# Attention scores from three products of 64 rows a head, two heads side by side on TensorE's row halves

## The chip, the cores and the metric

The kernel runs on one core of one Trainium2 chip. A core has a matrix engine (TensorE, "PE" in the profile), a vector engine (VectorE, "DVE"), an activation engine (ScalarE, "ACT"), a general engine (GpSimd, "POOL"), a queue engine that mostly issues DMAs (SyncE, "SP"), an on-chip memory of 128 partitions (SBUF) and eight accumulator banks (PSUM) into which TensorE writes. The metric is the device time of one execution in microseconds; smaller is better. Shown times are medians of several runs.

A product on TensorE loads a stationary operand (up to 128 rows of contraction by 128 columns) and streams a moving operand (the same rows by up to 512 columns) through it. "64 rows" below means that the contraction runs over 64 partitions only, so the product uses half of the array's rows; the other half can hold the stationary operand of another product. "Column halves" are the same thing for an output of 64 partitions.

## What is computed

Two layers of a transformer over 512 latent tokens and 256 context tokens, D = 1024. Layer 0 has 8 neighbourhood-attention heads (called NA) and 8 latent-attention heads (MLA) side by side, layer 1 has 16 sliding-window heads (SWA) that share 2 key/value heads. Cut to the attention scores:

```python
# NA (layer 0), head dim 64: near keys with a bias, and all context keys, in one softmax
s_lat = einsum('bnqhd,bknmhd->bhnqkm', qr, k_blk) * scale + bias;  s_ctx = einsum('bnqhd,bchd->bhnqc', qr, kc) * scale
# MLA (layer 0): 64 features of the head's own and 32 rotary ones, whose keys all heads share
sc = einsum('bqhc,bkc->bhqk', q_lat, c_kv) + einsum('bqhr,bkr->bhqk', q_rope, k_rope)
# SWA (layer 1): query head h uses key/value head h // 8; a sink logit per head joins the softmax
s_ctx = einsum('bqkgd,bckd->bkgqc', qg, kc) * scale;  s_lat = einsum('bqkgd,bmkd->bkgqm', qg, kb) * scale
```

Everything is float32. The kernel splits an operand x into a high part h (x rounded to TensorE's float32r type) and a low part l = x - h, and takes a product as h·h + l·h + h·l.

## The kernel before

**Stages.** Modulation vectors, the first input projections, then NA (about 197 to 275 us of the span), MLA (275 to 404 us), output projection and feed-forward of layer 0, then projections and SWA of layer 1 (about 1026 to 1178 us), output projection and feed-forward of layer 1. Inside a program stage the order on each engine comes from a scheduler that simulates the program and sorts by priority; a few stretches are ordered by hand, but not the attention.

**Attention jobs.** A job takes two lanes (for NA and SWA the two heads of a pair; for MLA two query groups of one head) through: scores into a PSUM bank of tag `s` (there are three), `take` (VectorE adds the bias, negates, copies to SBUF and keeps the minimum), `exps` (ScalarE), `turned` (transposes of 128x128 blocks by TensorE, copied back by VectorE and ScalarE), and `weighted`, the products with the values (L532 before, L531 after), where the lanes sit on the two column halves. Jobs overlap by one (`attend`), and side work (projections, finishing of pairs) is stepped between them. A query tile is 128 tokens, numbers 0 to 3 latent, 4 and 5 context.

**Scores of NA and SWA before** (`stacked_scores`, L745 and L746). A head's stationary operand is 128 rows: its 64 high rows and its 64 low rows, stacked. The moving operand is twice the head's keys: high over high, and low over low. So two products of 128 rows give all four terms. To make these, `put_q` writes high and low on different partition halves for each head, and `put_k` writes each key part twice, either by computing it again or by four DMAs a pair (`copies`).

**Scores of MLA before** (`latent_operands`, L1065 to L1067). A head's high tile holds its 64 own rows and 32 rotary rows, its low tile likewise; three products of 96 rows (head 0 of a pair) or 128 rows (head 1, with 32 rows of zeros). ScalarE and GpSimd build these tiles a head at a time (L1055, L1056), the rotary rows come by DMA on SP's queue.

**Queues.** All weight and bias loads and the on-chip copies named above are issued by `dma` (L134) on SP's queue, in the order that the scheduler gave. NA's bias tiles (`nb`) have two buffers, so a bias is loaded when the one before it has been read.

Of the kernel before, what the change touches and what calls it, by code (L numbers as in the profile page):

```python
# [10 lines left out]
F32R = mybir.dt.float32r  # L11
AF = mybir.ActivationFunctionType
ALU = mybir.AluOpType
# [42 lines left out]
ORDER = ("2", "n3", "m", "")  # L56
AFTER = "012k5678"
DBG = 0.43
KC = (0, 1, 0)
# [3 lines left out]
RK, RQ, RL, SQ = (2, 0), (0, 0), (0, 0), 1  # L63
# [37 lines left out]
def hybrid_kernel(ctx: ExitStack, tc, I, out):  # L101
# [443 lines left out]
    class Head:  # L545


        def __init__(self, side, scores, v, reach, bias, start, sums, mins):
            self.side, self.scores, self.v, self.reach, self.bias, self.start = side, scores, v, reach, bias, start
            self.dn = lambda q: sums[:, q, side : side + 1]  # L550
            self.mx = lambda q: mins[:, q, side : side + 1]
# [3 lines left out]
    def latent_lane(h, qs, blocks):  # L555

        sc = PS("s")
        for i, n in enumerate(qs):
            h.scores(sc[:, i * NX : (i + 1) * NX], n, CTXS)
        for i, n in enumerate(qs):  # L560
            a, z = h.reach(n)
            w = (z - a) * P
            s = PS("s")[:, :w]
            h.scores(s, n, slice(a * P, z * P))
            pt[0] += 1
            p = B(tag=PT[phase[0]][pt[0] % len(PT[phase[0]])])
            take(p, slice(w, w + NX), sc[:, i * NX : (i + 1) * NX], zeros.to_broadcast([P, NX]), h.start, h.mx(n))
            take(p, slice(0, w), s, h.bias(n), h.mx(n), h.mx(n))
            exps(p, slice(0, w + NX), h.mx(n), h.dn(n))
            for j, kt in enumerate([*range(a, z), 4, 5]):  # L570
                blocks[n, kt] = p[:, j * P : (j + 1) * P]
            yield True

    def near_lane(h, qs, blocks):

        for n in qs:
            s = PS("s")
            for at, key, w in NEAR[n]:
                h.scores(s[:, at : at + w], n, slice(key, key + w))
            pt[0] += 1  # L580
            p = B(tag=PT[phase[0]][pt[0] % len(PT[phase[0]])])
            take(p, slice(0, 512), s, h.bias(n), h.start, h.mx(n))
            exps(p, slice(0, 512), h.mx(n), h.dn(n))
            for j, kt in enumerate(NEAR_TILES[n]):
                blocks[n, kt] = p[:, j * P : (j + 1) * P]
            yield True

    def context_lane(h, qs, blocks):

        sc, p = PS("s"), B(tag="p")  # L590
        for i, n in enumerate(qs):
            c = slice(i * NX, (i + 1) * NX)
            h.scores(sc[:, c], n, CTXS)
            take(p, c, sc[:, c], zeros.to_broadcast([P, NX]), -LOWEST, h.mx(n))
            exps(p, c, h.mx(n), h.dn(n))
            for j in range(2):
                blocks[n, 4 + j] = p[:, i * NX + j * P : i * NX + (j + 1) * P]
        yield True

    def job(lanes, use, then=None):  # L600

        all_blocks = [{} for _ in lanes]
        for (h, qs), blocks in zip(lanes, all_blocks):
            yield from (context_lane if qs[0] > 3 else latent_lane if h.reach else near_lane)(h, qs, blocks)
        yield False
        o = PO()
        yield from weighted(o, [(h.v, blocks, qs) for (h, qs), blocks in zip(lanes, all_blocks)])
# [4 lines left out]
    def pair_jobs(hs, po, ctx_q, then):  # L612

        for qs in (((4, 5),) if ctx_q else ()) + ((0, 1), (2, 3)):
            c = slice(qs[0] * P, qs[0] * P + NX)
            yield job([(h, qs) for h in hs], lambda o, c=c: S.copy(po[:, c], o), then if qs[0] == 2 else None)

    def head_jobs(h, po, then):

        r = slice(64 * h.side, 64 * h.side + 64)  # L620
# [1284 lines left out]
```

## Time and profile before

| what | value |
|---|---|
| median of 3 runs | 1587.41 us (1586.18 to 1589.96) |
| the profiled execution: time, span | 1591.88 us, 1589.8 us |
| PE busy | 1536.5 us, 97% of the span |
| DVE, ACT, POOL busy | 1182.3, 806.8, 225.8 us |
| granted PE clock, mean | 0.992 |
| score products NA and SWA (L745, L746) | 216 and 216 |
| score products MLA (L1065, L1066, L1067) | 80 each |

The span is the time from the first to the last instruction that the profiler recorded; the execution's own time is 2.1 us longer. "Busy" counts a matmul until its modelled end, so neighbouring matmuls overlap and 97% does not mean that the array streams 97% of the time; start-to-start distances say how long a product holds the array.

### The profile page before, as it was taken

To read this page: it belongs to the slowest core of one execution; us is meant where nothing else is said; L and a number is where in the kernel's file an instruction comes from. 1 tells how busy PE (TensorE), PEld (TensorE's weight loads), DVE (VectorE), ACT (ScalarE), POOL (GpSimd) and SP (SyncE) were. 2 spreads that over 40 slices of the span, in tenths; PEclk is the share of its full clock that TensorE was granted. 3 is DMA by queue.
4 is the path that set the end of the run, shared out by engine and by line. 5 is a ranking of instruction groups with operands and counts; after the bars stand their busy time and mean duration, and the time that the engine had idled before them with its cause. 6 is when DMAs were issued, how large, how long until landed. Compare 5 with 4: busy or idle time off the path is not lost.

```text
span 1589.8 us, 26694 instructions
## 1 busy us (share of the span) xinstructions
PE 1536.5 (97%) x10034; PEld 1373.0 (86%) x10034; DVE 1182.3 (74%) x2365; ACT 806.8 (51%) x1643; POOL 225.8 (14%) x218
## 2 busy tenths in 40 slices
PE   6998989999999999999999999999999999999998
PEld 4686877787898989899999999878889998898997
DVE  4495968668589778785877776868877778687686
ACT  4364487677366324242333345557756545354463
POOL 0151724230010000000001010393002000000000
PEclk9999999999999999999999999999999999999999
DMA  9445343101562564746556555131006133233232
GB/s 342 148 162 192 102 125 101 36 11 64 180 208 86 163 233 154 240 144 214 199 191 243 194 208 207 41 104 43 2 14 198 40 108 128 87 100 114 90 103 87
DMA packets 80465, 214.93 MB, mean 135 GB/s; under 512 B 10192, under 2 KB 17872, under 8 KB 80336
## 3 DMA queue, kind: packets, MB, share of 16 engines
q1 hardware_dynamic: 73552, 188.05, 36.3%
q0 software_dynamic: 4480, 22.02, 3.6%
q10 hardware_dynamic: 2304, 3.15, 0.5%
q8 instruction: 79, 1.29, 0.3%
q14 instruction: 50, 0.41, 0.1%
HBM read 186.97 MB, written 23.07 MB: 132 GB/s over the span
## 4 chain that ended last, share of the span: by engine, by line
PE 76%; DVE 10%; DMA 7%; issue 3%; ACT 2%; POOL 2%; SPq 0%; DVEq 0%; ACTq 0%; POOLq 0%
PE pso L532 5%; PE pss L320 4%; PE pss L321 3%; PE pss L322 3%; PE pss L1343 3%; PE pss L1342 3%; PE pss L1341 3%; PE psd L320 3%; PE psd L321 3%; PE psd L322 3%; PE psd L1341 3%; PE psd L1343 3%; PE psd L1342 3%; PE pst L1343 3%; PE pst L1341 3%
## 5 line engine op out<-in xcount | busy, mean ns | idle before, releaser
L307 ACT CAST wh<-wr 128x512 fp32r<-128x512 f32 (+2 forms) x142 | 108.3, 777 | 196.3 <-DMA wr<-in_w_dn_dram 35.7
L308 DVE TENSOR_TENSOR wl<-wr,wh 128x1024 fp32r<-128x1024 f32 (+2 forms) x139 | 128.4, 931 | 75.4 <-ACT wh L307 74.8
L538 ACT ACTIVATE p<-p,sm 128x512 f32<-128x512 f32 (+3 forms) x144 | 105.1, 730 | 27.5 <-DVE sm L542 24.8
L215 DVE CUSTOM_DVE_ANT_0 p<-rope,cond 128x1024 bf16<-128x1024 f32 x64 | 77.5, 1222 | 29.8 <-DMA rope<-in_mod_w_dram 26.2
L321 PE MATMUL psd<-b,wh 128*128 128x256 f32 (+4 forms) x257 | 88.2, 343 | 0.0
L1343 PE MATMUL pss<-b,wl 128*128 128x256 f32 (+1 forms) x258 | 80.2, 311 | 4.2 <-DVE wl L1329 4.2
L1521 POOL DMA_DIRECT2D home<-p x40 | 21.6, 540 | 437.5 <-DVE p L1166 434.9
L1342 PE MATMUL pss<-b,wh 128*128 128x256 f32 (+1 forms) x258 | 80.0, 310 | 0.0
L320 PE MATMUL psd<-b,wh 128*128 128x512 f32 (+4 forms) x217 | 78.4, 361 | 1.4 <-ACT b L430 0.7
L1341 PE MATMUL pss<-b,wh 128*128 128x256 f32 (+1 forms) x258 | 79.6, 309 | 0.0
L320 PE MATMUL pss<-st,wh 128*128 128x256 f32 (+2 forms) x231 | 78.0, 338 | 0.4 <-ACT wh L307 0.4
L532 PE MATMUL pso<-ph,b 128*64 128x256 f32 (+1 forms) x384 | 78.1, 362 | 0.3 <-DVE ph L470 0.2
L532 PE MATMUL pso<-pl,b 128*64 128x256 f32 (+1 forms) x384 | 77.6, 362 | 0.7 <-DVE pl L470 0.7
L322 PE MATMUL pss<-st,wl 128*128 128x512 f32 (+2 forms) x231 | 77.8, 337 | 0.0
L322 PE MATMUL psd<-b,wl 128*128 128x512 f32 (+4 forms) x217 | 76.5, 353 | 0.0
L1343 PE MATMUL pst<-b,wl 128*128 128x384 f32 (+1 forms) x240 | 74.4, 311 | 0.3 <-DVE wl L1329 0.3
L1342 PE MATMUL pst<-b,wh 128*128 128x384 f32 (+1 forms) x240 | 74.4, 310 | 0.0
L1341 PE MATMUL pst<-b,wh 128*128 128x384 f32 (+1 forms) x240 | 74.4, 310 | 0.0
L321 PE MATMUL pss<-b,wh 128*128 128x256 f32 (+4 forms) x227 | 74.2, 328 | 0.1
L1342 PE MATMUL psd<-b,wh 128*128 128x384 f32 (+1 forms) x222 | 69.8, 314 | 0.0
L1341 PE MATMUL psd<-b,wh 128*128 128x384 f32 (+1 forms) x222 | 69.6, 314 | 0.0
L1343 PE MATMUL psd<-b,wl 128*128 128x384 f32 (+1 forms) x222 | 69.6, 314 | 0.0
(624 smaller groups left out, 5349.6 us busy)
## 6 DMA issues: line engine op xcount, KB each, us to landing
wr<-in_w_gu_dram SPq DMA_DIRECT2D x88, 512.0 KB, 4.2
rope<-in_mod_w_dram SPq DMA_DIRECT2D x48, 512.0 KB, 3.7
wr<-in_w_out_dram SPq DMA_DIRECT2D x32, 512.0 KB, 3.6
wr<-in_w_dn_dram SPq DMA_DIRECT2D x64, 256.0 KB, 2.8
p<-home SPq DMA_DIRECT2D x40, 384.0 KB, 3.9
home<-p POOLq DMA_DIRECT2D x40, 384.0 KB, 5.0
wr<-in_w_in_dram SPq DMA_DIRECT2D x21, 512.0 KB, 4.1
st<-in_mod_wp_dram SPq DMA_DIRECT2D x32, 256.0 KB, 4.7
```

The lines of the kernel that those rows point to most:

```text
L215: V.tensor_tensor_reduce(out=T("p", [P, D], mybir.dt.bfloat16), in0=w, in1=cond[:, v, :], op0=ALU.mult, op1=ALU.add, scale=1.0, scalar=0.0 ...
L307: S.copy(h, r)
L308: (G if eng else V).tensor_tensor(lo, r, f(h), op=ALU.subtract)
L320: PE.matmul(o, wh[:, k], mh[:, c], start=first and k == 0, stop=False)
L321: PE.matmul(o, wh[:, k], ml[:, c], start=False, stop=False)
L322: PE.matmul(o, wl[:, k], mh[:, c], start=False, stop=last and k == n - 1)
L532: ins = PE.matmul(o[64 * i : 64 * i + 64, c], v(kt), t, start=n == 0, stop=n == len(moving[i]) - 1)
L538: S.activation(p[:, c], p[:, c], AF.Exp, bias=nm, scale=-1.0, accum_out=dn)
L1341: PE.matmul(o, wh, xh, start=first and k == 0, stop=False, skip_group_check=not first)
L1342: PE.matmul(o, wh, xl, start=False, stop=False, skip_group_check=not first)
L1343: PE.matmul(o, wl, xh, start=False, stop=k == 3, skip_group_check=not first)
L1521: G.dma_start(home[m], t)
```

## The change

**NA and SWA.** Queries and keys of a pair of heads are kept as they come out of the projection: one tile with the high parts of both heads (head 0 in partitions 0 to 63, head 1 in 64 to 127) and one with the low parts (`halves`, `put_halves`). `pair_scores` takes three products of 64 rows a head (h·h, l·h, h·l), for the two heads in turn; head 0 uses the array's upper row half and head 1 the lower, and each writes a bank of its own. The helper `behind` keeps the six products in that order on TensorE, which allows other products between them. For SWA a pair is now head p with head p + 8, so that the two use different key heads; weights and sinks are rearranged to match.

**MLA.** Heads are now taken in pairs as in NA. The rotary part of a head is one product of 96 rows that comes first (`more`): the rotary rows as high, low and high against keys high, high and low. Then the same six products of 64 rows follow for the 64 own features. The high and low tiles are written directly from PSUM, and the rotary rows come in six DMAs a pair (`rotary_rows`).

**Around it.** Both heads of a pair now fill their banks together, two of the three `s` banks at a time. Three of the four NA pairs, not two, are split during the input projections; the fourth is split later (`split_pair`). No high or low part is written twice and `put_k`'s DMAs are gone; the tables that set which projection follows which (`ORDER`, `AFTER`) have fewer entries accordingly.

```diff
-    def stacked_scores(t1, ks):
-        def scores(o, q, keys):
-            x = t1[:, q * P : (q + 1) * P]
-            PE.matmul(o, x, ks[0][:, keys], start=True, stop=False)
-            PE.matmul(o, x, ks[1][:, keys], start=False, stop=True)
+    def pair_scores(qt, kt, more=None):
+        def scores(outs, q, keys):
+            q = slice(q * P, (q + 1) * P)
+            if more:
+                for o, x in zip(outs, more[0]):
+                    PE.matmul(o, x[:96, q], more[1][:96, keys], start=True, stop=False)
+            terms, run = ((0, 0), (1, 0), (0, 1)), []
+            for i, (x, y) in enumerate(terms):
+                for s, o in enumerate(outs):
+                    g = slice(64 * s, 64 * s + 64)
+                    ins = PE.matmul(o, qt[x][g, q], kt[y][g, keys], start=i == 0 and not more, stop=i == 2)
+                    run.append(behind(ins, *run[-1:]))
...
-    def near_lane(h, qs, blocks):
-        for n in qs:
-            s = PS("s")
-            for at, key, w in NEAR[n]:
-                h.scores(s[:, at : at + w], n, slice(key, key + w))
...
+    def near_lanes(hs, scores, qs, blocks):
+        for n in qs:
+            ss = [PS("s") for _ in hs]
+            for at, key, w in NEAR[n]:
+                scores([x[:, at : at + w] for x in ss], n, slice(key, key + w))
+            for h, x in zip(hs, ss):
+                p = new_p()
+                take(p, slice(0, 512), x, h.bias(n), h.start, h.mx(n))
+                exps(p, slice(0, 512), h.mx(n), h.dn(n))
...
-    def put_k(ks, copies=True, hi=None):
...
-                if copies:
-                    dma(k1[x, c], k1[r, c])
-                    dma(k2[x, c], k2[r, c])
-                else:
-                    moved(k1[x, c], src[r], 1.0, br)
-                    low(k2[x, c], src[r], k1[r, c], br)
+    def put_halves(t, scale=1.0, hi=None, lo=None):
+        def use(src, c, b=None):
+            h, l = t
+            if hi:
+                hi(h[:, c], src)
+            else:
+                moved(h[:, c], src, scale, b)
+            if b is not None:
+                V.scalar_tensor_tensor(l[:, c], src, b, f(h[:, c]), op0=ALU.add, op1=ALU.subtract)
+            elif scale != 1.0:
+                V.scalar_tensor_tensor(l[:, c], src, scale, f(h[:, c]), op0=ALU.mult, op1=ALU.subtract)
+            else:
+                (lo or V).tensor_tensor(l[:, c], src, f(h[:, c]), op=ALU.subtract)
...
-        for p in range(2):
-            yield from project_shifted(I["w_in0"][p], put_q(sets[p][0]), scale=0.125)
-            yield from project_shifted(I["w_in0"][p + 4], put_k(sets[p][1], KC[0]))
+        for p in range(3):
+            for i in range(2):
+                yield from project_shifted(I["w_in0"][p + 4 * i], put_halves(sets[p][i]), scale=(0.125, None)[i])
...
-    def latent_operands(h):
...
+    def rotary_rows(p):
+        q3.append([T("st", [P, NT], F32R) for _ in range(2)])
+        for s, t in enumerate(q3[p]):
+            h = 2 * p + s
+            rr = slice(32 * (h % 4), 32 * (h % 4) + 32)
+            for i in range(3):
+                dma(t[32 * i : 32 * i + 32], QR[h // 4][i % 2][rr, :NT])
```

**Where it moves instructions.** Three places, as the built programs order them. A row is one instruction (line, operation, output<-inputs, output shape; `x2` for two equal ones in a row).

TensorE in SWA. Before, L745 and L746 are a head's two score products of 128 rows, L479 the transposes:

```order
L745 MATMUL pss_11508<-st_10402,st_10633 128x384
L746 MATMUL pss_11508<-st_10403,st_10633 128x384
L479 MATMUL pst_11494<-ident_r_88,p_11451 128x128
L479 MATMUL pst_11515<-ident_r_88,p_11451 128x128
L479 MATMUL pst_11494<-ident_r_88,p_11474 128x128
L479 MATMUL pst_11515<-ident_r_88,p_11474 128x128
L479 MATMUL pst_11515<-ident_r_88,p_11451 128x128
L479 MATMUL pst_11515<-ident_r_88,p_11474 128x128
L745 MATMUL pss_11528<-st_10402,st_10634 128x256
L746 MATMUL pss_11528<-st_10403,st_10634 128x256
```

The same stage in the change. L727 are products of 64 rows, in turn into the banks of the two heads (`pss_11369` head 0, `pss_11370` head 1), L478 the transposes, L531 the products with the values:

```order
L531 MATMUL pso_10832<-pl_11299,b_10520 64x256 x2
L727 MATMUL pss_11338<-st_10444,st_10575 128x256
L727 MATMUL pss_11337<-st_10444,st_10576 128x256
L727 MATMUL pss_11338<-st_10444,st_10576 128x256
L727 MATMUL pss_11337<-st_10445,st_10575 128x256
L727 MATMUL pss_11338<-st_10445,st_10575 128x256
L727 MATMUL pss_11369<-st_10444,st_10618 128x256
L478 MATMUL pst_11401<-ident_r_88,p_11276 128x128
L478 MATMUL psd_11408<-ident_r_88,p_11276 128x128
L478 MATMUL psd_11424<-ident_r_88,p_11276 128x128 x2
L478 MATMUL pst_11417<-ident_r_88,p_11278 128x128
L727 MATMUL pss_11370<-st_10444,st_10618 128x256
```

Two products of 128 rows became six of 64 rows for two heads; here the first product of head 0 stands apart from head 1's, with transposes between them.

TensorE in MLA. Before, three products of a head after the transposes:

```order
L479 MATMUL psd_3881<-ident_r_88,p_3800 128x128
L1065 MATMUL pss_3931<-st_3044,st_3046 128x512
L1066 MATMUL pss_3931<-st_3044,st_3047 128x512
L1067 MATMUL pss_3931<-st_3045,st_3046 128x512
L1065 MATMUL pss_3943<-st_3044,st_3046 128x256
```

In the change L722 is a head's rotary product of 96 rows, L727 those of 64 rows:

```order
L722 MATMUL pss_3496<-b_2467,st_3141 128x512
L727 MATMUL pss_3496<-st_3102,st_3104 128x512
L478 MATMUL psd_3406<-ident_r_88,p_3240 128x128
...
L478 MATMUL pst_3413<-ident_r_88,p_3246 128x128
L722 MATMUL pss_3497<-b_2467,st_3142 128x512
L727 MATMUL pss_3497<-st_3102,st_3104 128x512
L727 MATMUL pss_3496<-st_3102,st_3105 128x512
L727 MATMUL pss_3497<-st_3102,st_3105 128x512
```

Head 0's first product of 64 rows stands between its rotary product and transposes; head 1 follows later, when the run of five closes both.

SP's queue in NA. Before, the key copies of the fourth pair (`st_...<-st_...`) stand among the bias loads of the second pair:

```order
L134 DMA nb_2126<-in_nb_dram 128x768
L134 DMA st_2292<-st_2292 64x768
L134 DMA nb_2127<-in_nb_dram 128x768
L134 DMA st_2293<-st_2293 64x768
L134 DMA st_2294<-st_2294 64x768
L134 DMA st_2295<-st_2295 64x768
L134 DMA nb_2130<-in_nb_dram 128x768
```

In the change the bias loads follow each other there; the rotary rows of MLA's first pair come later, ahead of the last pair's bias (`nb_2773`):

```order
L133 DMA nb_2770<-in_nb_dram 128x768
L133 DMA st_2732<-b_2728 32x768 x2
L133 DMA st_2732<-b_2729 32x768
L133 DMA st_2733<-b_2728 32x768
L133 DMA st_2733<-b_2729 32x768
L133 DMA st_2733<-b_2728 32x768
L133 DMA nb_2773<-in_nb_dram 128x768
```

Counted over the whole program: score products are 672 before (all of 96 or 128 rows), and in the change 80 of 96 rows and 888 of 64 rows. The 888 stand in 148 unbroken runs. The number of places where TensorE goes from one kind of product to another kind (all rows and columns, row halves, column halves, column quarters) is 152 before and 416 in the change.

257 lines of the change are left out of this document (99 added, 158 removed).

## The prediction

> **What bounds the kernel now.** I read the page's busy line and the chain that ended last first, then the stretches of the attention stages.
>
> ```profile
> PE 1536.5 (97%) x10034; PEld 1373.0 (86%) x10034; DVE 1182.3 (74%) x2365; ACT 806.8 (51%) x1643; POOL 225.8 (14%) x218
> ...
> PE 76%; DVE 10%; DMA 7%; issue 3%; ACT 2%; POOL 2%; SPq 0%; DVEq 0%; ACTq 0%; POOLq 0%
> ```
>
> The same by stretch (microseconds; busy time and instructions of PE, weight loads, DVE, ACT, POOL; then clock, DMA share, GB/s): input projections, NA, MLA, the end of SWA's projections, SWA.
>
> ```profile
> 95.00:197.00 102.00, 97.32 (x593) 77.29 (x591) 78.95 (x139) 50.22 (x115) 48.80 (x36) 0.98 0.46 149
> 197.00:275.00 78.00, 71.05 (x542) 57.88 (x541) 60.62 (x153) 63.48 (x150) 26.47 (x20) 1.00 0.37 108
> 275.00:404.00 129.00, 126.65 (x939) 101.63 (x938) 90.00 (x248) 91.18 (x207) 27.54 (x18) 1.00 0.18 60
> 1060.00:1090.00 30.00, 27.68 (x185) 22.43 (x186) 24.76 (x75) 18.75 (x42) 22.38 (x16) 0.94 0.35 124
> 1090.00:1178.00 88.00, 86.93 (x721) 70.62 (x719) 74.72 (x262) 66.37 (x166) 5.30 (x5) 1.00 0.01 1
> ```
>
> MLA and SWA are TensorE's: PE has 126.65 of 129 us and 86.93 of 88, DVE 70% and 85%. There each 0.1 us on TensorE is 0.1 us of the end. NA has slack (71 of 78).
>
> **The score products.** Their count by width is in the two forms of L745 (L746 has the same) and in L1065 (L1066 and L1067 too).
>
> ```profile
> L745 PE MATMUL pss<-st,st x194: 211/337/562, 197.2 to 1169.9; 128*128 128x256 f32 x132, 128*128 128x384 f32 x32, 128*128 128x192 f32 x12, 128*128 128x64 f32 x12
> L745 PE MATMUL pss<-b,b x22: 214/359/497, 228.0 to 251.5; 128*128 128x256 f32 x12, 128*128 128x192 f32 x4, 128*128 128x64 f32 x4, 128*128 128x512 f32 x2
> L1065 PE MATMUL pss<-st,st x80: 277/363/504, 274.9 to 384.9; 96*128 96x256 f32 x24, 128*128 128x256 f32 x24, 96*128 96x512 f32 x16, 128*128 128x512 f32 x16
> ```
>
> What one holds the array is the distance to the next start, in the order of time:
>
> ```profile
> 318.20 0.40 PE L1067 MATMUL pss<-st,st 96*128 96x512 f32 x1
> 318.43 0.28 PE L1065 MATMUL pss<-st,st 128*128 128x256 f32 x1
> 318.55 0.28 PE L1066 MATMUL pss<-st,st 128*128 128x256 f32 x1
> ```
>
> 0.23 us for 512 columns, 0.118 for 256 (from more of such rows), 0.174 between them for 384; a 192 and a 64 count as one 256. The first two rows also show that 128 rows follow 96 at no price. L745 is 144 at 0.118, 32 at 0.174, 16 at 0.118 and 8 at 0.231: 26.3 us, with L746 52.6. L1065 is 48 and 32: 13.1 us, three lines 39.2. Together 91.8 us.
>
> In the change the 96-row products take 13.1. The 64-row products are three a head; if two heads share the array, a call lasts three widths where two heads took four (NA, SWA): 39.5 us, and in MLA 19.6. But in the order 28 of MLA's 40 calls, and some of the others, have head 0's first product alone: such a width is lost, 5.1 us in MLA and 3.0 elsewhere. Sum 80.3 us, of which 67.2 for the 64-row products: **streams -11.5 us** (-19.6 if no product were alone).
>
> **Do halves share the array, and what does going there cost?** No row here has 64 rows. The nearest are the products with the values, on column halves:
>
> ```profile
> 321.34 0.28 PE L320 MATMUL psd<-b,wh 128*128 128x256 f32 x1
> 321.45 0.28 PE L321 MATMUL psd<-b,wh 128*128 128x256 f32 x1
> 321.66 0.43 PE L532 MATMUL pso<-ph,b 128*64 128x256 f32 x1
> 321.67 0.43 PE L532 MATMUL pso<-pl,b 128*64 128x256 f32 x1
> 321.93 0.38 PE L532 MATMUL pso<-ph,b 128*64 128x256 f32 x1
> 321.94 0.38 PE L532 MATMUL pso<-pl,b 128*64 128x256 f32 x1
> 322.15 0.38 PE L532 MATMUL pso<-ph,b 128*64 128x256 f32 x1
> ...
> 324.09 0.38 PE L532 MATMUL pso<-ph,b 128*64 128x256 f32 x1
> 324.10 0.38 PE L532 MATMUL pso<-pl,b 128*64 128x256 f32 x1
> 324.40 0.39 PE L322 MATMUL psd<-b,wl 128*128 128x256 f32 x1
> 324.63 0.28 PE L1065 MATMUL pss<-st,st 128*128 128x256 f32 x1
> 324.75 0.28 PE L1066 MATMUL pss<-st,st 128*128 128x256 f32 x1
> ```
>
> Two halves start 0.01 us apart, every 0.215 us: 12 products, two passes each, in 12 steps. A product that is alone makes its two passes one after the other:
>
> ```profile
> 281.09 0.65 PE L532 MATMUL pso<-ph,b 128*64 128x256 f32 x2
> 281.67 0.66 PE L479 MATMUL pst<-ident_r,p 128*128 128x128 f32 x4
> ```
>
> So column halves do overlap, and I take row halves to do so too. The first rows give the price of the change of kind. Going in: 321.45 to 321.66 is 0.21 instead of 0.118, and 321.66 to 321.93 0.27 instead of 0.215: 0.15. Coming out: 324.09 to 324.40 is 0.31 instead of 0.215, and 324.40 to 324.63 0.23 instead of 0.118: 0.21 here, 0.16 where transposes follow. I take 0.155 a switch. The change has 416 switches for 152, so 264 more: **switches +40.9 us**, between 0 (the 96-to-128 rows) and 264 at 0.18, 47.5. By stage the extra is 52 in NA, 122 in MLA, 89 in SWA. I take the upper row, since a half is what changes there too, while 96 rows and 128 use one array.
>
> The Trainium skill (TensorEngine Tiling (Array Packing), Key Properties) says that a change of tiling mode, not a change of tile within it, drains TensorE. The column rows agree with it at 0.15 us; that it holds for row halves no run here shows. By that rule all 264 switches cost, and it speaks against this change. Its TensorE: Matmul & The Clock Gate, Measured speedup, has four row tiles at 3.07 times one, 77% of full sharing; by that figure, an estimate, the 67.2 us of 64-row products would be 87 and the end 1626 us.
>
> **Cover in NA.** TensorE's waits by stretch (total us, times, longest):
>
> ```profile
> PE pst L320 <- DVE st L716: 2.9, 2, 1.6
> ...
> PE psd L320 <- DVE st L716: 0.3, 1, 0.3
> ...
> PE pss L745 <- DVE sm L542: 5.4, 5, 2.4
> ```
>
> The last is NA's: takes that wait for bias loads. NA's 52 switches (8.1 us) partly fall into such waits: **-4 us** (0 to -8).
>
> **Operands.** Rows by form: count, then busy us and mean ns.
>
> ```profile
> L716 DVE SCALAR_TENSOR_TENSOR st<-pst,sm,st 64x512 fp32r<-64x512 f32 x8 | 6.0, 748 | 2.4 <-ACT st L432 2.3
> ...
> L1055 ACT CAST st<-b 64x768 fp32r<-64x768 f32 x16 | 13.3, 828 | 3.2 <-PE pss L1066 2.9
> L1056 POOL TENSOR_TENSOR st<-b,st 64x768 fp32r<-64x768 f32 x16 | 29.6, 1853 | 66.3 <-ACT st L1055 65.9
> L702 POOL TENSOR_TENSOR st<-b,st 64x512 fp32r<-64x512 f32 x16 | 24.2, 1514 | 31.3 <-ACT st L701 30.6
> ...
> 140.00:150.00 10.00, 9.30 (x52) 6.62 (x53) 1.26 (x7) 0.38 (x2) 0.01 (x1) 0.83 0.66 246
> ```
>
> In the projections a key pair cost DVE 8 such steps and a query pair 4; now 2 and 2, for three pairs. The 3.2 us that PE waited for L716 (2.9, and 0.3 on another bank) go, and with them perhaps the clock of 0.83 over 10 us behind these pauses (1.7): **-5 us** (0 to -6). What is late next there are DVE's modulation sums, which are spread between.
>
> In MLA ACT loses L1055 and POOL L1056; DVE gains 16 low parts at 0.48 or 0.75 (9.8 us, on 90 of 129). All lie under TensorE: zero, and still zero if PE were 10 us shorter. In SWA's projections POOL does half of L702's steps; PE is idle 2.3 us of 30 there: **-1 us** (0 to -2.3).
>
> SP's queue: the fourth pair's key copies blocked it, and the second pair's biases behind them:
>
> ```profile
> 214.52 4.18 SPq L134 DMA_DIRECT2D st<-st  x3
> ...
> L134 SPq DMA_DIRECT2D st<-b x16: 507/539/593, 268.7 to 333.8; - x16
> ```
>
> They are gone (up to -4.2). In their place six rotary copies (24 in all, for 16) stand ahead of the last NA bias: 6 at 0.54 is +3.2 at most, and more if the rotation they wait for is late. **-1 us.**
>
> **Sum:** -11.5 + 40.9 - 4 - 5 - 1 - 1 = +18.4. The profiled execution took 1591.9 (span 1589.8), so 1610.3; it lies 4.5 above the median, so **1606 us** against 1587.4.
>
> **Rivals.**
> 1. *Switching to row halves is cheap* (the other side: faster). Place: the 148 runs of 64-row products. For it: 96 and 128 rows alternate free of charge. Against: every change of columns costs 0.15. At no price: -11.5 - 7 = -18.5, 1569 us; it decides from below 18.5 / 264 = 0.07 us a switch. 27%.
> 2. *Row halves do not share the array*, so that the change does not do what it says. The 64-row products one after the other take 118.1 us for 67.2: +50.9, 1657 us. For it: no row of its kind; against: column halves. 8%.
> 3. *Banks become the bound.* A call now fills two of three banks, so head 1 of the next waits for a take, and what stands behind it in TensorE's order waits too:
>
> ```profile
> 328.31 0.74 DVE L542 CUSTOM_DVE_ANT_0 p<-pss,zeros,sm 128x512 f32<-128x512 f32 x1
> ```
>
> 28 split MLA calls at half of that are +10: 1616 us. Against: in MLA takes end with transposes and values products to fill in. 9%.
>
> **How the numbers follow.** The forecast has 50% (its own range 1592 to 1628: switches at 0.12 to 0.18, offsets from nothing to 15 us). Rival 1 27%, rival 2 8%, rival 3 9%. A price near 0.07, which ends within 0.2% (3.2 us, what a measurement of this kernel can tell from none), 6%. So faster 0.28 (rival 1 and a percent of the forecast's low end), same 0.06, slower 0.66. The range 1568 to 1632 leaves out rival 2 and the lower part of rival 1.
>
> **What would show it.** Right: in the order of time, two 64-row products starting 0.01 us apart; the start after a product of another kind 0.09 late and the next 0.06; MLA's stretch near 146 us, SWA's near 95. No wait on L716's place in the projections. Wrong: starts at 0.03 to 0.12 across the kinds (rival 1), 64-row products 0.118 apart one by one (rival 2), or long waits of score products for DVE's takes (rival 3).

## The result

The changed kernel takes 1638.6 us (median of 4 runs) beside 1586.8 for the kernel before: 1.0313 times, interval 1.0285 to 1.0341. That is 51.8 us slower, where 18.4 were forecast. Slower was right, 1606 us was not, and the time lies above the range. The profiled execution took 1634.4 us (span 1632.3; before 1591.9 and 1589.8). The four runs of the change part by the clock that TensorE was granted: 1630.7 and 1634.4 us at 0.991, 1642.9 and 1645.0 at 0.983 and 0.985.

The page of the changed kernel, busy time and the chain that ended last:

```profile
PE 1572.7 (96%) x10298; PEld 1367.0 (84%) x10298; DVE 1168.4 (72%) x2358; ACT 767.4 (47%) x1576; POOL 173.0 (11%) x185
...
PE 53%; DVE 9%; DMA 6%; issue 6%; ACT 1%; SPq 0%; DVEq 0%; ACTq 0%; POOLq 0%
```

PE is 36 us busier. The chain says less: its shares add up to 75% here and to 100% before, because in the change it is followed back only to 383 us of the span, so PE's 53% cannot be set beside the 76% before. By stretch (columns as in the prediction): projections, NA, MLA to the last score product, SWA's first calls, SWA.

```profile
95.00:190.00 95.00, 94.71 (x598) 76.83 (x596) 69.44 (x127) 41.43 (x102) 50.56 (x37) 1.00 0.49 152
190.00:281.00 91.00, 83.77 (x666) 61.63 (x665) 59.04 (x152) 59.12 (x147) 12.50 (x11) 0.92 0.28 88
281.00:413.00 132.00, 130.71 (x859) 87.66 (x861) 86.39 (x247) 67.03 (x159) 0.00 (x0) 1.00 0.17 52
1053.00:1097.00 44.00, 39.26 (x189) 29.41 (x187) 23.30 (x51) 17.84 (x29) 35.52 (x25) 0.96 0.38 131
1097.00:1226.00 129.00, 117.00 (x1008) 84.75 (x1009) 89.49 (x309) 76.41 (x193) 3.87 (x3) 1.00 0.01 1
```

Before, the first two were 102 and 78 us long (their rows stand in the prediction); the other three, of the kernel before:

```profile
275.00:386.00 111.00, 110.29 (x828) 88.64 (x827) 75.77 (x223) 79.71 (x184) 27.54 (x18) 1.00 0.10 28
1035.00:1076.00 41.00, 37.95 (x185) 30.94 (x185) 27.50 (x60) 21.92 (x37) 39.08 (x26) 0.98 0.37 126
1076.00:1179.00 103.00, 101.93 (x839) 82.37 (x837) 85.67 (x300) 76.07 (x191) 12.15 (x10) 0.99 0.02 8
```

So the projections gave 7 us back, NA took 13 more, MLA 21, and SWA with its first calls 29. That is more than the 42 us between the two profiled executions: to its last product with values MLA is only 12.6 longer (145.5 for 132.9), and what follows SWA is 5 us shorter. In NA and MLA PE is busy for nearly all of what was added (13 of 13 and 20 of 21). NA also ran at a clock of 0.92 where it was 1.00; 8% of 91 us is 7 us, an estimate of what that can have cost at most. In SWA's last stretch it is busy for 15 of 26: here PE waits, though DVE has only 89 of 129 us to do. The waits of PE for takes, and of DVE for scores, over the whole kernel (total us, times, longest); first the change, then the kernel before:

```profile
PE pss L727 <- DVE sm L541: 13.0, 15, 2.5
...
DVE p L541 <- PE pss L727: 55.4, 40, 4.1
DVE p L541 <- DMA nb<-in_nb_dram: 12.7, 7, 3.3
DVE wr L541 <- PE pss L727: 9.3, 6, 3.3
```

```profile
PE pss L745 <- DVE sm L542: 7.1, 7, 2.4
...
DVE p L542 <- PE pss L746: 11.7, 11, 2.6
...
DVE p L542 <- PE pss L1067: 9.3, 9, 3.3
...
DVE wr L542 <- PE pss L1067: 2.4, 5, 0.8
```

DVE waits for score products nearly three times as long (65 us for 23), and PE for takes nearly twice as long. Where it happens is seen in the groups of SWA's stretch; the group is the takes of context scores, the last column DVE's idle time just before them. The kernel before (from 1075 us) and the change (from 1097):

```profile
L542 DVE CUSTOM_DVE_ANT_0 p<-pss,zeros,sink_neg 128x256 f32<-128x256 f32 x56 | 24.7, 478 | 0.1
```

```profile
L541 DVE CUSTOM_DVE_ANT_0 p<-pss,zeros,sink_neg 128x256 f32<-128x256 f32 x56 | 23.8, 481 | 27.7 <-PE pss L727 27.7
```

The switches are seen in the order of time. A visit to the row halves in SWA, and a split call in MLA, in the change:

```profile
1099.52 0.44 PE L478 MATMUL psd<-ident_r,p 128*128 128x128 f32 x2
1099.89 0.98 PE L727 MATMUL pss<-st,st 64*128 64x256 f32 x12
1100.80 0.55 PE L478 MATMUL pst<-ident_r,p 128*128 128x128 f32 x3
1101.18 0.60 PE L478 MATMUL psd<-ident_r,p 128*128 128x128 f32 x4
1101.62 0.60 PE L478 MATMUL pst<-ident_r,p 128*128 128x128 f32 x4
```

```profile
333.43 0.50 PE L722 MATMUL pss<-b,st 96*128 96x512 f32 x1
333.86 0.96 PE L727 MATMUL pss<-st,st 64*128 64x512 f32 x5
334.75 0.39 PE L722 MATMUL pss<-b,st 96*128 96x256 f32 x1
335.07 0.38 PE L727 MATMUL pss<-st,st 64*128 64x256 f32 x1
335.38 0.38 PE L740 MATMUL psd<-wh,b 128*128 128x256 f32 x1
335.60 0.28 PE L741 MATMUL psd<-wl,b 128*128 128x256 f32 x1
```

Twelve products of 256 columns in 0.91 us: six widths of 0.118 are 0.71, so the halves do share the array, and 0.20 is the price inside the visit. The three transposes behind it take 0.38; by the next four (0.44 from 1101.18 to 1101.62) 0.33 is theirs. The two ahead of it take 0.37 for 0.22, of which some 0.05 belong to the way out of the column halves before them. That makes some 0.34 a visit. In MLA the 96-row product of 512 columns holds the array 0.43 instead of 0.23 when a 64-row product follows. The product at 335.07 has nothing beside it: it costs 0.20 to reach (0.32 for 0.118), 0.118 for itself, 0.19 to leave (0.31 for 0.118), and 0.10 more on the step behind.

### The profile page after: what moved, and what is told of

It is laid out like the page before. It is cut to its first block, busy times and chain, and to the rows that moved or that the text cites. A ratio compares the mean times of both kernels' runs of the same rounds, so it can differ in the third digit from the quotient of the medians.

```text
span 1632.3 us, 27095 instructions
## 1 busy us (share of the span) xinstructions
PE 1572.7 (96%) x10298; PEld 1367.0 (84%) x10298; DVE 1168.4 (72%) x2358; ACT 767.4 (47%) x1576; POOL 173.0 (11%) x185
## 4 chain that ended last, share of the span: by engine, by line
PE 53%; DVE 9%; DMA 6%; issue 6%; ACT 1%; SPq 0%; DVEq 0%; ACTq 0%; POOLq 0%
PE pss L1296 3%; PE pso L531 3%; DMA wr<-in_w_gu_dram 3%; PE pss L1294 3%; PE pss L1295 3%; PE psd L319 3%; PE pss L319 3%; PE pss L320 3%; PE pss L321 3%; PE psd L321 3%; PE psd L320 3%; PE pst L1296 2%; PE pst L1294 2%; PE pst L1295 2%; PE psd L1294 2%
## 5 line engine op out<-in xcount | busy, mean ns | idle before, releaser
L306 ACT CAST wh<-wr 128x512 fp32r<-128x512 f32 (+3 forms) x142 | 108.4, 777 | 206.2 <-PE psd L1295 33.6
L307 DVE TENSOR_TENSOR wl<-wr,wh 128x512 fp32r<-128x512 f32 (+3 forms) x139 | 129.3, 935 | 87.8 <-ACT wh L306 87.5
L727 PE MATMUL pss<-st,st 64*128 64x256 f32 (+4 forms) x822 | 108.7, 341 | 13.4 <-DVE sm L541 13.0
L727 PEld LDWEIGHTS pss<-st,st 64*128 64x128 f32 x822 | 69.1, 192 | 46.9 <-DVE sm L541 21.0
L531 PE MATMUL pso<-pl,b 128*64 128x256 f32 (+1 forms) x368 | 80.3, 374 | 1.9 <-ACT pl L470 1.7
L531 PE MATMUL pso<-ph,b 128*64 128x256 f32 (+1 forms) x368 | 82.0, 376 | 0.0
L1294 PE MATMUL psd<-b,wh 128*128 128x384 f32 (+1 forms) x222 | 69.9, 315 | 0.0
```

What stands on the lines that cost most here:

```text
L306: S.copy(h, r)
L307: (G if eng else V).tensor_tensor(lo, r, f(h), op=ALU.subtract)
L531: ins = PE.matmul(o[64 * i : 64 * i + 64, c], v(kt), t, start=n == 0, stop=n == len(moving[i]) - 1)
L727: ins = PE.matmul(o, qt[x][g, q], kt[y][g, keys], start=i == 0 and not more, stop=i == 2)
L1294: PE.matmul(o, wh, xh, start=first and k == 0, stop=False, skip_group_check=not first)
```

## The experiments

Fifteen kernels were run. The differences are to the kernel before on the same chip. "Switches" is how often TensorE's order changes between full rows, row halves and column parts. "Rows" is how the 64-feature score products run: stacked (as before), halves, or full rows (all 128 rows of a pair's tiles). "Clock" is the mean granted TensorE clock of the runs. It matters: with each kernel's own mean taken out, a run that was granted 0.001 less took 1.1 us longer (the slope over all these runs). Each edit also lets the scheduler order the stages anew; the differences include that.

| kernel | heads fill banks | rows | switches | median, us | to before, us | ratio, interval | clock |
|---|---|---|---|---|---|---|---|
| before | in turn | stacked | 152 | 1587 to 1589 | | | 0.994 |
| the change | in pairs | halves | 416 | 1638.6 | +51.8 | 1.0313 (1.0285 to 1.0341) | 0.988 |
| e1 | in pairs | full, 2 a head | 134 | 1602.9 | +15.4 | 1.0096 (1.0079 to 1.0114) | 0.991 |
| e2 | in pairs | full, 3 a pair | 134 | 1590.2 | +2.7 | 1.0017 (1.0003 to 1.0032) | 0.989 |
| e3, one run a call | in pairs | halves | 361 | 1625.3 | +37.8 | 1.0229 (1.0209 to 1.0250) | 0.988 |
| e4, four banks | in pairs | halves | 407 | 1668.0 | +80.6 | 1.0503 (1.0481 to 1.0525) | 0.979 |
| e5 | in turn | full, 2 a head | 134 | 1572.5 | -15.4 | 0.9894 (0.9876 to 0.9912) | 0.994 |
| e6, e1 with takes by head | in pairs | full, 2 a head | 134 | 1605.4 | +17.5 | 1.0104 (1.0087 to 1.0120) | 0.989 |
| e7, more switches | in pairs | halves | 713 | 1702.7 | +114.8 | 1.0717 (1.0696 to 1.0739) | 0.977 |
| e8, e3 with takes by head | in pairs | halves | 365 | 1624.5 | +36.6 | 1.0233 (1.0211 to 1.0254) | 0.988 |
| e9, e1 with four banks | in pairs | full, 2 a head | 146 | 1638.1 | +50.1 | 1.0314 (1.0290 to 1.0338) | 0.985 |
| e10, key copies by DMA | in turn | stacked | 152 | 1583.1 | -4.9 | 0.9978 (0.9961 to 0.9995) | 0.993 |
| e11, the same on POOL's queue | in turn | stacked | 152 | 1582.2 | -5.9 | 0.9961 (0.9945 to 0.9977) | 0.994 |
| e12, e1 with copies moved | in pairs | full, 2 a head | 134 | 1589.5 | +1.6 | 1.0007 (0.9990 to 1.0024) | 0.992 |
| e13, the change with copies moved | in pairs | halves | 420 | 1620.0 | +30.7 | 1.0201 (1.0173 to 1.0229) | 0.988 |
| e14, e3 with copies moved | in pairs | halves | 365 | 1609.7 | +20.3 | 1.0126 (1.0100 to 1.0152) | 0.989 |
| e15, e11 with copies moved | in turn | stacked | 154 | 1577.6 | -11.7 | 0.9939 (0.9913 to 0.9964) | 0.994 |

### The three parts of the change: e1, e2 and e5

The change does three things at once: cheaper operands, two heads filling banks in pairs, and row halves. e1 takes the row halves away:

```diff
-            terms, run = ((0, 0), (1, 0), (0, 1)), []
+            terms, run = ((0, 0), (1, 0)), []
...
-                    g = slice(64 * s, 64 * s + 64)
-                    ins = PE.matmul(o, qt[x][g, q], kt[y][g, keys], start=i == 0 and not more, stop=i == 2)
+                    ins = PE.matmul(o, qt[x][:, q], kt[y][:, keys], start=i == 0 and not more, stop=i == 1)
```

> The pairs of heads, their banks, the operands and the order of calls are those of the change, but each 64-row product is replaced by a product over all 128 rows, two a head: as many widths a call as before the change, and no product on row halves (the score becomes a sum over both heads, and the third product is left out). Switches between kinds: 134 (before 152, after 416). Theory 1 (the switches are the loss; the pairing costs nothing): the kernel before plus the cheaper operands, 1587 less 7, about 1580 us, and no more waiting of score products for takes than before (13 us). Theory 2 (filling two of three banks at once is the loss besides): the waits that the change added in NA and SWA, some 13 us, stay without the row halves: about 1593 us.

e2 keeps three products a call (the first and the third for one head's bank, the second for the other's):

> As the run before, but three full-row products a call in place of the six on halves: the widths that the change has where both halves are filled, without one switch (of three products two go to one head's bank and one to the other's or the other way round, so the scores are not those of the reference). Theory 1: about 20 us of score products less than with four products a call, so near 1560 us; the change would have been a gain but for its switches. Theory 2: the shorter products only lengthen the waits for takes, 1575 to 1590 us.

e5 is e1 with the pairing undone too:

```diff
-        yield from (context_lanes if qs[0] > 3 else latent_lanes if hs[0].reach else near_lanes)(hs, scores, qs, blocks)
+        for h in hs:
+            alone = lambda outs, n, keys, s=h.side: scores(outs, n, keys, (s,))
+            yield from (context_lanes if qs[0] > 3 else latent_lanes if hs[0].reach else near_lanes)([h], alone, qs, blocks)
...
```

> The run with four full-row products a call (e1_full_rows_4, 1602.9 us), with one thing undone: the two heads' scores are made one head after the other, each call filling one bank, as before the change. Same products, operands and number of banks; the scores are sums over both heads and lack the third product. Theory 2 (pairing the banks is what made e1 15 us slower than the kernel before): the 17 us of waits that e1 has more in SWA go, 1580 to 1586 us. Rival (the pairing is innocent, and the operands or the order of the side work make SWA slower): within 3 us of 1603.

e1 came out at +15.4, above what either theory gave; e2 at the upper end of what theory 2 gave; e5 at -15.4, 8 us below the lower end of what theory 2 gave. The products of e5 and e1 are the same in number and width as those of the kernel before, so the steps can be read off:

- **Operands** (before to e5): -15 us.
- **Pairing** (e5 to e1): +31 us.
- **Row halves** (e1 to the change): +36 us.

The sum is 52, the 51.8 measured. Two other things lie inside these parts. e5 has 18 switches fewer than the kernel before, some 3 us of its 15 at the prediction's price. And the mean clock falls with each of the last two steps, from 0.994 in e5 to 0.991 and 0.988: at 1.1 us for 0.001 some 3 us of the 31 and 4 of the 36, an estimate. What lowers the clock was not tried by a run of its own. The pairing acts in SWA. Its stretch in e1 and in e5, and the same group of takes:

```profile
1068.00:1197.00 129.00, 117.01 (x895) 89.72 (x897) 89.63 (x309) 76.15 (x193) 3.62 (x3) 1.00 0.01 1
...
L541 DVE CUSTOM_DVE_ANT_0 p<-pss,zeros,sink_neg 128x256 f32<-128x256 f32 x56 | 23.8, 481 | 28.7 <-PE pss L726 28.7
```

```profile
1059.00:1162.00 103.00, 102.26 (x852) 83.57 (x852) 87.54 (x307) 76.66 (x193) 3.88 (x3) 1.00 0.04 15
...
L541 DVE CUSTOM_DVE_ANT_0 p<-pss,zeros,sink_neg 128x256 f32<-128x256 f32 x58 | 25.6, 480 | 0.0
```

Without row halves the pair shows the same 129 us and the same 28 us of idle DVE as the change; with heads in turn both are gone. From e1 to e2 the score products get 20 us shorter and the kernel only 12.7. That the waits for takes swallow the rest, as theory 2 had it, is not seen: PE waits 14.0 us for them in e2 and 16.9 in e1. The clock, 0.002 lower in e2, can be some 3 us of it.

By stretch, in the profiled executions, the row halves (e1 to the change) cost 9.7 us in NA (up to 4 of it the clock's, 0.92 for 0.96), 19.2 in MLA, where the clock is 1.00 in both, and 1.1 in SWA. In SWA the switches fill time in which PE waited anyway: its gaps beyond streams and switches, from all its starts in order of time, are 25 us in e1 and 16 in the change.

### The price of a switch: e7 and e3

e7 adds one product of 64 columns on all rows among the six of each call:

```diff
+                if i == 1:
+                    ins = PE.matmul(outs[0][:, :64], qt[0][:, q], kt[0][:, keys.start : keys.start + 64], start=False, stop=False)
+                    run.append(behind(ins, run[-1]))
```

> The change with one small product on all 128 rows (64 columns, 0.05 us) put among the six of every call, so that each call leaves the row halves once more: 713 switches in place of 416; 114 more products have nothing beside them. It adds into head 0's scores, which are not those of the reference. Small products 7 us, lost widths up to 13. Theory 1 (each switch has its price, wherever it stands): 297 at 0.16 to 0.20 us, 48 to 59 us more, so 1694 to 1718 us. Rival (the time goes with the waits for banks, and switches disappear in them): 1645 to 1660 us.

It is 63 us slower than the change (by the differences to the kernel before), inside theory 1's range. Less 7 for the small products and 0 to 13 for the lost widths, 43 to 56 us are left for 297 switches, 0.14 to 0.19 us each. But not all of that is the switches' own. NA in e5, e1 and e7, and SWA in e7 (the change has 0.92 over NA's 91 us, and 0.99 over the 173 of SWA):

```profile
190.00:265.00 75.00, 70.67 (x565) 58.74 (x565) 56.98 (x152) 57.96 (x147) 14.24 (x11) 1.00 0.33 100
189.00:270.00 81.00, 74.40 (x567) 61.78 (x566) 57.37 (x149) 57.31 (x143) 13.26 (x11) 0.96 0.31 94
190.00:308.00 118.00, 113.61 (x723) 83.33 (x722) 62.73 (x155) 61.06 (x149) 11.93 (x11) 0.83 0.22 68
1113.00:1293.00 180.00, 172.80 (x1144) 118.98 (x1142) 103.26 (x346) 89.31 (x212) 24.33 (x18) 0.92 0.07 24
```

The share of the clock that was not granted, times the length, is 20 us in NA and 14 in SWA for e7, and 7 and 2 for the change: up to 25 of the 68 us between the two profiled executions are the lower clock, an estimate. Without them a switch comes to about 0.1 us over the whole kernel, so that e7 fell into theory 1's range is in part luck. The price itself is read where no wait and no lower clock blurs it: from e1 to the change MLA takes 19.2 us for 135 more switches, **0.14 us each**, and single visits show up to **0.19**. Two calls of three widths in e7, with the small products (L730) between:

```profile
1182.44 0.30 PE L730 MATMUL pss<-st,st 128*128 128x64 f32 x1
1182.67 0.62 PE L727 MATMUL pss<-st,st 64*128 64x256 f32 x6
1183.22 0.30 PE L730 MATMUL pss<-st,st 128*128 128x64 f32 x1
1183.45 0.56 PE L727 MATMUL pss<-st,st 64*128 64x256 f32 x3
```

A small product holds the array 0.23 us for some 0.05, six products 0.55 us for 0.354: 0.38 for two switches.

The Trainium skill (TensorEngine Tiling (Array Packing), Key Properties) says that changing the tiling mode drains TensorE, and changing the tile within a mode does not. The trace agrees for row halves in the time it takes: the visit to them at 1099.89 has 0.20 us more inside and 0.05 behind it, and the halves alternate within it at no price, since visits of twelve products and of six both have 0.20 more.

e3 keeps a call of MLA in one piece by chaining the 96-row products ahead of the six:

```diff
-                for o, x in zip(outs, more[0]):
-                    PE.matmul(o, x[:96, q], more[1][:96, keys], start=True, stop=False)
+                for s in (0, 1):
+                    ins = PE.matmul(outs[s], more[0][s][:96, q], more[1][:96, keys], start=True, stop=False)
+                    run.append(behind(ins, *run[-1:]))
...
```

> The change, with the 96-row products of both heads at the head of the same run, so that no other product comes between head 0's first product and the rest. Switches 416 to 361, products with nothing beside them 80 to 26. Theory 1: 55 switches at 0.16 to 0.2 us and some 50 lost widths, mostly of 512 columns in MLA, at 0.13 to 0.23: 8.8 to 11 and 6.5 to 11, about 1620 us; MLA's stretch 15 us shorter. Theory 2: the wait for the second bank only moves to the first product, at most 5 us gained, 1632 to 1638 us.

14 us faster than the change, where theory 1 gave about 18 and theory 2 at most 5; MLA's stretch, to its last product with values, is 134.4 us for 145.5. A call as it now runs, the six products (L729) taking 0.55 us from 331.91 for three widths of 0.118:

```profile
331.62 0.36 PE L724 MATMUL pss<-b,st 96*128 96x256 f32 x1
331.91 0.62 PE L729 MATMUL pss<-st,st 64*128 64x256 f32 x6
332.46 0.50 PE L724 MATMUL pss<-b,st 96*128 96x256 f32 x2
```

So theory 1 holds for the switches where PE has no waits. It does not hold for the whole: e1 and e5 show the pairing beside them.

### Why pairs make SWA wait: e4, e6, e8, e9, e12 and e13

Three reasons were open: the third bank, the order in which takes free a bank, and bursts on DVE, which gets four takes at once and then none. e4 gives the scores a fourth bank, at the cost of one of the two banks of the up projections (tag `d`):

```diff
-PBUFS = dict(s=3, t=2, o=1, d=2)
+PBUFS = dict(s=4, t=2, o=1, d=1)
...
```

> The change, with four PSUM banks for scores in place of three (one for the up projections in place of two). Switches 407. Theory 1: 9 switches less, 1.6 us, nothing else: about 1635 us. Theory 2: a call no longer waits for a take of the call before it; the 16 us by which the waits exceed the forecast go for the most part: 1620 to 1628 us.

Both theories missed: NA's stretch grew from 91 to 106 us and MLA's from 146 to 165. The up projections have one bank less there, and the clock is 0.81 in NA and 0.97 in MLA (0.92 and 1.00 in the change), which can be some 13 and 5 us of it, by the same estimate as for e7. Only SWA answers the question: less the projections beside it, it went from 138.4 to 135.0. e9 asks the same without row halves:

> e1_full_rows_4 with four banks for scores and one for the up projections, as in e4. What counts is the SWA stretch, where the up projections have no part: from its first score product to its last values product, less the projections beside it, it took 137.8 us in e1 (25 us of waits) and 114.6 in e5 (6 us). If the third bank is what the pair lacks: 116 to 122 us. If the loss lies in the bursts (a call of two heads gives VectorE four takes at once and then none, so that VectorE and TensorE wait for each other in turn), a fourth bank helps by a few us: 128 to 135 us. The whole, with NA and MLA slowed as in e4: 1610 to 1625 us.

SWA's stretch less its projections is 128.6 us (162.1 less 33.5), at the near end of the range given for bursts: 9 of the 23 us between e1 and e5. The whole is slower than expected, for NA and MLA as in e4 (NA at a clock of 0.88).

e6 and e8 let head 0's context bank go after two takes:

```diff
-        for i, n in enumerate(qs):
-            for h, x in zip(hs, sc):
+        for h, x in zip(hs, sc):
+            for i, n in enumerate(qs):
                 a, z = h.reach(n)
```

> e1_full_rows_4 with the context takes of MLA and SWA in another order: both of head 0, then both of head 1, so that head 0's bank is free after two takes in place of three; heads still fill banks in pairs. If score products wait for that bank: one take of 256 columns (0.48 us) less in each of the 16 SWA jobs, 5 to 8 us, 1595 to 1598 us. If the wait is for the third bank or for the takes as a whole: 1600 to 1605 us.

> e3_one_run_a_call (1625.3 us) with the context takes by head: the two mends together. Switches 365. Theory 1 and 2 each right for its part: the bank is free a take earlier in SWA, 5 to 8 us: 1617 to 1620 us. If the takes' order doesn't matter where switches lengthen the products: 1623 to 1627 us.

Neither moved (+2.1 to e1 and -1.2 to e3, within the spread): the order of the takes in a burst is not what PE waits for.

e12 makes the burst shorter. It moves copies of transposed blocks in SWA from VectorE to ScalarE:

```diff
-COPY = ("vva", "vvva", "vva")
+COPY = ("vva", "vvva", "vaa")
```

> e1_full_rows_4 (pairs of heads, full-row products, 1602.9 us) with one of the two VectorE copies in three of transposed blocks moved to ScalarE in SWA: of 51 copies there about 25, some 16 us of VectorE's 90 in that stretch, for 14 us more on ScalarE (76 of 129). The banks and their order stay. If TensorE waits because VectorE has takes and copies in one burst: 5 to 10 us less, 1593 to 1598 us. If only the number of banks counts: 1600 to 1606 us.

VectorE's copies in SWA go from 54 to 27. It is 13.8 us faster than e1, with the same banks in the same order, and more than expected. e13 does the same to the change itself:

> The change (1638.6 us) with the copies of transposed blocks in SWA moved as in e12 (from VectorE two in three to one in three). Switches 420. If the burst on VectorE is in the change too, beside the switches: 8 to 13 us less, 1626 to 1631 us. If the switches cover it (SWA takes 173 us with row halves and 172 with full rows): within 3 us of 1638.

21 us faster than the change, twice what was expected. The profiled execution of e13 is the slowest of its runs, at a clock of 0.985 (0.991 in that of the change), and shows only 8.6 of them; there SWA takes 129.6 us less its projections for 138.4. The stretch in e13 and its wait for takes, and that wait in the change's stretch from 1097 us:

```profile
1080.00:1212.00 132.00, 125.44 (x1028) 90.33 (x1027) 84.73 (x312) 97.04 (x234) 18.23 (x14) 0.97 0.09 28
...
PE pss L727 <- DVE sm L541: 3.7, 2, 2.5
```

```profile
PE pss L727 <- DVE sm L541: 6.1, 10, 1.1
```

PE is idle 6.6 us of 132 there (12 of 129 in the change), and its wait for takes is 3.7 in 2 pieces for 6.1 in 10. So in the change too part of what PE waits for in SWA is that DVE has takes and copies to do together. A timeline of e1 shows such a burst: four takes from 1104.40 to 1106.1, after an idle time of 2.43 us, three copies until 1107.7, and only then the next takes.

```profile
1104.40 0.48 DVE L541 CUSTOM_DVE_ANT_0 p<-pss,zeros,sink_neg 128x256 f32<-128x256 f32 x1 [2.43 <-PE pss L726]
...
1106.03 0.56 DVE L469 COPY pl<-psd 128x384 f32<-128x384 f32 x1
1106.50 1.28 DVE L469 COPY ph<-pst 128x512 f32<-128x512 f32 x2
1107.69 0.48 DVE L541 CUSTOM_DVE_ANT_0 p<-pss,nb,sm 128x256 f32<-128x256 f32 x1
```

The two remedies were not tried together. Each leaves SWA 12 to 14 us above e5's 114.6 (126.2 in e12), so how the rest divides between bank and burst stays open.

### Both mends, and a version that beats both: e14, e10, e11 and e15

> e3_one_run_a_call (1625.3 us) with the copies moved too: both mends, each seen alone before. Switches 365. If they add: 1612 to 1617 us. What is then left above the kernel before is the price of row halves at 126 visits: more than 20 us slower still.

1609.7, a little under the expected 1612 to 1617: the mends add to within 4 us (31 of 14 and 21), and 20 us above the kernel before are left. Row halves at 126 visits do not pay here: e12, with pairs and moved copies too, but full rows and no third product, is at +1.6.

The operands were worth 15 us without the pairs. e10 takes the part of that which the kernel before can have as it stands, with `put_k`'s second copies written by DMA in the projections, and e11 puts these DMAs on POOL's queue:

```diff
-KC = (0, 1, 0)
+KC = (1, 1, 0)
...
-                    dma(k1[x, c], k1[r, c])
-                    dma(k2[x, c], k2[r, c])
+                    q = nc.sync if b is None else G
+                    q.dma_start(f(k1[x, c]), f(k1[r, c]))
+                    q.dma_start(f(k2[x, c]), f(k2[r, c]))
```

> The kernel before, with the second copies of the keys of the first two pairs written by DMA in place of ScalarE and VectorE: the VectorE steps of a key pair in the projections 8 to 4. The change saved 7 us there. If those waits of TensorE are VectorE's operand steps: 3 to 6 us faster than before, 1581 to 1585 us. If the copies on SP's queue hold up the weights behind them: no gain or slower, 1587 to 1592 us.

> As e10, with these copies on POOL's queue, away from the weights: if VectorE's steps are the cause and SP's queue a danger, 1580 to 1585 us and better than e10; if POOL's own work in the projections (49 of 102 us) holds them up until NA waits for its keys, no better than the kernel before.

Both are faster than the kernel before, by 4.9 and 5.9 us, and not told apart from each other. The projections of e10:

```profile
95.00:188.00 93.00, 93.00 (x588) 75.62 (x587) 74.24 (x131) 44.80 (x105) 47.86 (x35) 1.00 0.59 180
```

PE is busy for all 93 us, where it was 97.3 of 102; the clock is 1.00 for 0.98, and SP's queue took the copies without harm.

> e11_keys_by_pool_dma (1582.2 us, heads one after the other, full rows) with the copies moved: the control. Without pairs TensorE waits for a take 1.7 us in SWA, so there is little to gain: 1579 to 1584 us. If instead VectorE's load is a cost of its own in SWA, whatever the order of the heads: 1570 to 1576 us.

1577.6 us, 11.7 less than the kernel before on its chip: the fastest of the versions that leave nothing out. The result lies between its two ranges. SWA's stretch is as long as in e11 (142.0 and 142.5 us in the profiled executions), so what the copies add over e11 is not located, and the intervals overlap. Of the 14 and 21 us of e12 and e13 up to 6 may thus be worth having without pairs too.

## Why the prediction was wrong, step by step

- **The step that failed is the one on the banks.** The sum had the pairing at nothing; rival 3 gave it +10 us, placed in MLA, as something that would come in place of the forecast. It is a term of the sum, measured at +31 us, and its place is SWA (29 of the 34 us that it takes in the profiled executions, 23 without the projections beside it; 6 in NA, and none in MLA, whose last product with values comes 126.3 us after its start for 127.3). The stretches that the prediction named say the same: MLA was to grow by 17 us (129 to 146) and grew by 12.6, SWA's last stretch was to grow by 7 (88 to 95) and grew by 26. The argument against banks, that MLA has other products to fill in, holds for MLA. It was carried over to SWA, where DVE stood at 74.7 of 88 us in the prediction's own rows and takes come with copies. Fed evenly, DVE at 83% of SWA's stretch hid behind PE; fed in bursts, at 69% of a longer one, it did not.
- **Row halves.** That two share the array was right: products of a pair start within 0.01 us of each other. A switch at 0.155 us was near the mark: 0.14 in MLA, up to 0.19 in e7's calls, and near 0.25 for the single product beside 96-row ones above. Streams came out at -9 us for -11.5 (all score products' own widths, in order of time). Switches and streams together were forecast at +29.4, or 32 for the 282 switches between e1 and the change; the measured part is +36, some 4 of it the clock's.
- **Price between 96 rows and 64.** The rows had 96 to 128 rows free, and the forecast priced 96 to 64 as any other change. That was right (0.20 us), and rival 1, which took these rows for a hint of cheap switches, fell.
- **The cover in NA (-4).** There was none: NA grew by 13 us, and PE is idle there for 7.2 us where it was 7.0, so the switches came on top. The lower clock, up to 7 of the 13, is a term that the sum did not have. DVE's takes waited for bias loads 12.7 us in 7 waits; in this stretch before it was

```profile
DVE wr L542 <- DMA nb<-in_nb_dram: 4.9, 4, 3.3
```

  In e5 (in turn) it is 2.4 and in e1 (in pairs) 4.5, so pairs alone do not lengthen this wait. Why it is longer in the change was not tried by a run, and it does not show in PE's idle time.
- **Operands.** -7 forecast (projections, SWA's projections, SP's queue); the projections' stretch gave 7.1 us, with the waits on L716's place gone and the clock at 1.00, as forecast. The whole, in e5, is -15: NA and MLA too are some 3 and 6 us shorter there. 14 switches fewer in MLA are some 2 us of its 6; how the rest came about was not tried. The forecast had the operands of MLA at zero because PE covered them.
- **SP's queue (-1).** The six rotary copies do stand ahead of the last bias, for 3.8 us (3.2 forecast):

```profile
268.56 3.76 SPq L133 DMA_DIRECT2D st<-b  x6
272.42 0.53 SPq L133 DMA_DIRECT2D nb<-in_nb_dram  x1
```

- **Rival 2** fell with the pairs' starts. By the Trainium skill's figure for four row tiles (TensorE: Matmul & The Clock Gate, Measured speedup vs the span model) the 64-row products would have taken 87 us, an estimate. With two halves the trace shows full sharing, 0.118 us for a pair.

So +18.4 became +51.8 by 31 for the pairing, 11 for the row halves (36, where 29.4 less 4 of cover were forecast), and 8 less for the operands (-15 for -7): 34 together, for 33.4. The lower clock, 0.988 for 0.994, runs through these parts with some 7 us, an estimate at 1.1 us for 0.001.

One number of the range was off by itself: the upper end of the forecast's own range, 1628, counts from the profiled execution (1591.9 and 36), where the forecast counts from the median, which gives 1623. The measured time lies above both.

## What to carry to other kernels

Count an array mode's switches before its saved columns: at 0.14 to 0.19 us a switch a visit costs some 0.34 us, and a call of three widths in place of four saves 0.12 to 0.23. Such packing needs long runs, not many. And whenever two producers are made to run side by side, ask what their consumer sees: an engine that was fed evenly and now gets its work in bursts can hold the others up without a single instruction more (DVE has 2358 in e1 and in e5), and moving half of its copies is a cheap way to find out. When two runs differ, look at the granted clock before the difference is put down to the edit.

## What the runs showed that was not expected

- Row halves share fully for two heads, yet TensorE's own gain, 9 us of streams, is a fifth of what getting there and back costs (some 45 us: the 36 measured and the 9 gained, for 282 switches more than e1).
- Where TensorE waits in short pieces, as in SWA with pairs, switches are nearly free (1.1 us for 91 more of them), and where it does not, as in MLA, they cost their full price (19.2 us for 135 more). Counts are by the order of time.
- Moving 27 copies of 0.55 to 0.68 us off DVE, some 17 us, made e12 14 us faster and e13 21, though DVE was busy for only 89 of 129 us. Up to 6 of these 14 and 21 us came without pairs too.
- The granted clock falls in step with the edits: 0.994 before and with heads in turn, 0.991 in pairs, 0.988 with row halves, 0.977 with more switches. The runs do not say why.
